# The last group's down projection takes banks of both PSUM pools, and a pair of transfers and tiles is moved at its start

## The chip, the cores and the metric

The kernel runs on one core of a Trainium2 chip. The metric is the device time of one execution in microseconds. TensorE (PE) multiplies, VectorE (DVE), ScalarE (ACT) and GpSimd (POOL) do the rest, and SyncE (SP) issues nearly all transfers. PSUM has eight banks, each of which holds one 128 x 512 product in fp32. Data lies in SBUF with 128 partitions; sizes of tiles below are bytes in one partition.

## The reference, cut to what matters

One layer of a hybrid encoder: 16 meta tokens and 2048 frames, model width 1024. After the mixers (a recurrent part and an attention part) and their output projection `w_o`, the layer ends in a convolutional feed-forward block, which is what the change is about:

```python
h = h + concat([y_rw, y_fx]) @ w_o
h = h + conv_ffn(rmsnorm(h, norm2_g), ffn_w_in, ffn_conv_w, ffn_conv_b, ffn_w_out)

def conv_ffn(x, w_in, conv_w, conv_b, w_out):   # w_in 1024 x 5632, w_out 2816 x 1024
    h = x @ w_in
    y = conv_b + sum(conv_w[i] * shifted(h, 2 - i) for i in range(3))   # causal, by channel
    u, gt = split(y, 2)
    return (silu(gt) * u) @ w_out
```

All is fp32. The kernel writes each operand as a high and a low part in fp32r (`hi` is a cast on ACT, `lo` the difference on DVE or POOL) and multiplies hi x hi, hi x lo and lo x hi, so that each product of 128 x 128 by 128 x 512 is three matmuls.

## The kernel before

The tokens are laid out with features in partitions. The feed-forward block goes by four groups of 512 tokens (`FGROUPS`): `early[0]` and `early[1]` one after the other, and the last two, `a` and `b`, together by a scheme with fewer products (class `Last`). `tail` (L1442) sets the order: `w_o` of `early[1]`, its feed-forward (`F.mlp`), then `w_o(a)`, `half_a`, `w_o(b)`, and `rest()`, which is the last down projection of `early[1]` (L1227): eight products into banks `pr`, each followed by an add on DVE into `acc` (L1237) and by the transfer of that 256 KB piece to the output (L1240).

The last group works on 22 pairs of weight blocks `f`. `Last.up(f)` (L1308) loads two weight tiles `raw` (L1312), makes sums and differences of their quarters (`s1` on POOL, L1342, and three more on POOL, in place), splits them (`qh`, `ql`, L1322 and L1323; `rh`, `rl`, L1348), and forms products of them with seven operands. Of these p1, p2 and ra come from group a alone. p5 (`t1h`, `t1l`), p6 (`t2`), p4 (`t4`), p7 (`t3`), p3 (`b2`) and rb need group b, and `half_b` (L1284) makes them: eight scalings by the norm's factor `rs`, four sums and differences of 128 x 1536, and a cast on ACT and a difference on DVE for each. `rs` comes from a power and a spread on POOL (L1173, L100) and transposes on TensorE (L103). The sums of products are A, B, D and Cb in four banks `pr`; DVE adds them, and the convolution and the gate follow on ACT and DVE (L1338, L1340, L1400, L1402), with the result z split by ACT and POOL (L1404, L1405).

`Last.down` (L1408) multiplies two blocks z by their output weights: 16 products of six matmuls, each into a bank of `self.out` and then added by DVE into `acca` or `accb` (L1423); it is called 11 times, one call for each two `f`, in `Last.mlp` (L1427), behind the matmuls of the next `up`. Its weights use the same `raw` and `qh`, `ql` tiles (two buffers each) as the up projection. In the last call each add is followed by the transfer to the output (L1425).

PSUM is divided into `ffpA`, three banks `pp`, and `ffpR`, five banks `pr`. Before, the last group's up projection has `pr` and its down projection `pp`.

SBUF on the left side is a stack. During the early groups it holds `ffe`, `ffw` (two `ww_raw`, three `ww_hi`, three `ww_lo`, 4096 each), `ffA` (`acc`, 8 x 514 x 4 = 16,448), `ffB` (`xh`, 16,448), `ffC` (`xl`), `ffD`. When they are closed, the same space is given to `ffL0` (late operands of `half_b`: those named in `late_ops`, 6144 each, and `rh`, `rl`, 4096 each), `ffV` (M.W: `raw` first, then `s1`, `qh`, ...), and `ffL1` (the other operands). Group b's attention output lies in `xh` and `xl` (`yB`, L1478) until `w_o(b)` has read it. A tile that gets space of an earlier one waits for all of that one's readers.

Nothing here is ordered by hand alone: the program is traced in the order of the calls, and the scheduler of the language (`schedule_with_timeline_sim=True`, L1550) puts each engine's instructions, and each queue of transfers, in an order that it takes from a simulated timeline. Within an engine and a queue the order is then fixed, and an instruction that waits holds up those behind it.

Of the kernel before, what the change touches and what calls it, by code (L numbers as in the profile page):

```python
# [62 lines left out]
def pools(*args):  # L63

    *ps, where = args
    return lambda shape, tag, bufs=1, dt=F32: ps[where.get(tag, -1)](shape, tag, bufs, dt)
# [1031 lines left out]
class Ffn:  # L1098
# [128 lines left out]
    def down(self, G, fs, zs):  # L1227
        K, nc, acc = self.K, self.K.nc, G.acc
        w = [self.weight(K.fout[f]) for f in fs]
        for m in range(KC):  # L1230
            ms = slice(128 * m, 128 * m + 128)
            for b, nb in G.blocks:
                p = G.out([128, 512])[:, :nb]
                self.product(p, [(wh[:, ms], wl[:, ms], zh[:, b : b + nb], zl[:, b : b + nb])
                                 for (wh, wl), (zh, zl) in zip(w, zs)])
                a = acc[:, m, b : b + nb]
                nc.vector.tensor_tensor(a, a, p, op=ALU.add)  # L1237
            if fs[-1] == FT - 1:
                s = max(16 - G.T0, 0)
                nc.sync.dma_start(K.outT[m, :, G.T0 + s - 16 : G.T0 - 16 + G.n], acc[:, m, s : G.n])  # L1240

    def mlp(self, G, switch=FT, out=None):

# [198 lines left out]
def tail(K, ctx, at, c0):  # L1442

    tc = K.tc
    edge = Pool(tc, ctx, "ffe", side="left")
    late = ExitStack()
    ctx.enter_context(late)
    pA = Pool(tc, ctx, "ffpA", PSUM, side="left")
    bank = lambda shape: pA(shape, "pp", 3)
    turn = ExitStack()  # L1450
    with ExitStack() as c1:
        W = Pool(tc, c1, "ffw", side="left")
        F = Ffn(K, W, (3, 2), edge)
        gA = pools(*(Pool(tc, c1, f"ff{i}", side="left") for i in "ABCD"), {"acc": 0, "xh": 1, "xl": 2})
        cvA = lambda: gA([128, 512], "cv", 5)
        early = [F.group(*g, dict(x=gA, a=gA, z=gA, out=bank, up=bank, ytag="x", abufs=1, parts=WHOLE, small=KC,
                                  cv=cvA, sq=cvA, stage=lambda i: lambda c: cvA())) for g in FGROUPS[:2]]
        early[0].parts = PARTS
        early[0].small = KC // 2
        early[1].small = 0  # L1460
        early[1].last = True
        F.w_o(early[0])
        at(1, False)
        c0.close()
        with ExitStack() as c2:
            attention(K, c2, "at2", [[[2 * i, 2 * i + 1] for i in range(4, 8)]], (1, 4, 2, 352, 2, 0, 0), (2, 2, 1))(0, False)
        pR = Pool(tc, late, "ffpR", PSUM, side="right")
        bankR = lambda shape: pR(shape, "pr", 5)
        F.mlp(early[0])()
        F.w_o(early[1])  # L1470
        rest = F.mlp(early[1], 8, bankR)
        R = Pool(tc, late, "ffR", side="right")
        T = Pool(tc, turn, "ffT", side="right")
        tn = ExitStack()
        N = Pool(tc, tn, "ffN", side="right")
        yA = lambda: [Thirds([R([128, cs.stop - cs.start, 512], f"p{i}", dt=F32R) for i, cs in zip(t, CH3)])
                      for t in ((0, 1, 4), (2, 3, 5))]
        yB = lambda: [gA([128, KC, 514], "x" + t, dt=F32R) for t in "hl"]  # L1478
        a, b = (F.group(*g, dict(x=N, a=R, atag=t, y=y, abufs=1, out=bankR, up=bank, parts=WHOLE, small=KC,
                                 sq=lambda: N([128, 512], "sqv", 1)), win=True)  # L1480
                for g, t, y in zip(FGROUPS[2:], ("acca", "accb"), (yA, yB)))
        M = Last(F, a, b)
        F.w_o(a)
        M.half_a(R, T)
        F.w_o(b)
        rest()

    late_ops = ("t4h", "t4l", "t3h", "t3l", "b2h", "b2l", "rh", "rl")
    L0 = Pool(tc, late, "ffL0", side="left")
    M.W = Pool(tc, late, "ffV", side="left")  # L1490
    L = pools(L0, Pool(tc, late, "ffL1", side="left"), dict.fromkeys(late_ops, 0))
    tn.close()
    with ExitStack() as c1:
        U = Pool(tc, c1, "ffU", side="right")
        M.first = M.up(0)
        next(M.first)
        M.half_b(L, Pool(tc, c1, "ffB", side="left"), T, U)
    turn.close()
    M.C = Pool(tc, late, "ffC2", side="left")
    M.Z = Pool(tc, late, "ffZ", side="right")  # L1500
    M.bank, M.out = bankR, bank
    M.mlp()


# [9 lines left out]
def trunk(tc, args, out, shapes):  # L1514
    K = SimpleNamespace(nc=tc.nc, tc=tc, outT=out, **args)
    with ExitStack() as c0:
        dr = Pool(tc, c0, "scratch", DRAM)
        for name, shape in SCRATCH.items():
            setattr(K, name, dr(list(shape), "d_" + name))
        setup(K, c0)  # L1520
        with ExitStack() as c:
            mixer = ExitStack()
            c.enter_context(mixer)
            at = None
            with ExitStack() as c1:
                def first():
                    nonlocal at
                    mixer.close()
                    at = attention(K, mixer, "at", [[[-1, 0, 1], [2, 3]], [[4, 5], [6, 7]]], (2, 3, 3, 544, 3, 1, 0), (2, 2, 1))
                    at(0, True)  # L1530

                phase1(K, c1, mixer, rwkv, first)
            tail(K, c, at, mixer)
# [21 lines left out]
```

## Time and profile before

| | |
|---|---|
| three timed runs | 3402.91, 3417.93 and 3419.29 us, median 3417.93 |
| profiled execution | 3404.62 us, of which the span of the instructions is 3402.8 us |
| busy share of the span | PE 96%, PEld (weight loads, beside PE) 85%, DVE 69%, ACT 49%, POOL 34% |
| the chain that ended last | PE 48%; DVE 4%; DMA 3% |
| the last group's up and down projections | from about 2662 us to the end |
| transfers of 256 KB to the output | 2.4 to 2.5 us to landing |

The page gives the shares over the whole span; they are averages over stages with different limits. The views by stretch (busy time of each engine, count of its instructions, granted TensorE clock as a share of 2.4 GHz, share and rate of the DMA engines), of waits, and of the timeline show a single stage. In a timeline, consecutive equal instructions are merged; the bracket gives how long the engine was idle before the first of them and what released it.

### The profile page before, as it was taken

Reading aid. Unit: us, or ns where it says so; the run is one execution under the profiler, and the core shown is the slowest. Engines: PE = TensorE matmul, PEld = TensorE weight load, DVE = VectorE, ACT = ScalarE, POOL = GpSimd, SP = SyncE. Lnnn points to the kernel's source line nnn. Section 1 sums busy time; section 2 is a strip of 40 time slices with the busy share of each in tenths; the row PEclk is TensorE's granted clock in tenths of the full one; section 3 lists DMA queues with packets and bytes.
Section 4 is the critical chain, followed back from the end, with each engine's and each line's share of the span. In section 5 each row is a group of like instructions: output and inputs, shape, how many; then the busy total and the mean of one; then the engine's idle time right before and its main releaser. Section 6 shows DMA issues by size and latency. Waiting matters only on the chain.

```text
span 3402.8 us, 61891 instructions
## 1 busy us (share of the span) xinstructions
PE 3275.4 (96%) x23061; PEld 2906.4 (85%) x23061; DVE 2352.7 (69%) x4946; ACT 1664.9 (49%) x3529; POOL 1159.8 (34%) x1733
## 2 busy tenths in 40 slices
PE   7999999999999999999999999999999899999999
PEld 7889888988988988999999998888888677777777
DVE  5665666566556757887878886777665677667666
ACT  5542444554244457765666665654343343334342
POOL 4441112444111157755445453412014422222221
PEclk9999999999999999999999999999999899999999
DMA  4566333356634255333233344324233111111112
GB/s 111 122 133 154 105 93 102 99 121 133 158 88 108 78 172 162 116 107 111 80 89 100 94 130 132 94 73 158 94 98 115 65 50 50 41 53 56 38 50 87
DMA packets 346517, 341.93 MB, mean 100 GB/s; under 512 B 168376, under 2 KB 281256, under 8 KB 345192
## 3 DMA queue, kind: packets, MB, share of 16 engines
q1 hardware_dynamic: 346024, 337.91, 35.1%
q8 instruction: 182, 2.98, 0.4%
q14 instruction: 119, 0.97, 0.1%
q0 software_dynamic: 192, 0.07, 0.0%
HBM read 267.62 MB, written 70.27 MB: 99 GB/s over the span
## 4 chain that ended last, share of the span: by engine, by line
PE 48%; DVE 4%; DMA 3%; ACT 2%; issue 2%; POOL 2%; SPq 0%; ACTq 0%; POOLq 0%; DVEq 0%
PE pp L1121 23%; PE pr L1121 16%; PE o L1031 3%; PE pt L1011 3%; DMA raw<-d_qk 2%; PE s L961 1%; PE s L963 1%; DVE v L1340 1%; DVE rl L1349 1%; DMA raw<-in_fin_dram 1%; POOL kl L903 0%; ACT P L980 0%; ACT ph L1026 0%; DVE ql L89 0%; DVE c L1331 0%
## 5 line engine op out<-in xcount | busy, mean ns | idle before, releaser
L82 DVE TENSOR_TENSOR ww_lo<-ww_raw,ww_hi 128x1024 fp32r<-128x1024 f32 (+1 forms) x172 | 215.5, 1260 | 79.1 <-ACT ww_hi L81 45.0
L1121 PE MATMUL pp<-xh,ww_hi 128*128 128x256 f32 (+2 forms) x1248 | 248.3, 326 | 4.3 <-ACT xh L1186 3.2
L1121 PE MATMUL pp<-xh,ww_lo 128*128 128x256 f32 (+2 forms) x1248 | 250.3, 325 | 0.0
L1121 PE MATMUL pp<-xl,ww_hi 128*128 128x256 f32 (+2 forms) x1248 | 247.9, 324 | 0.0
L81 ACT CAST ww_hi<-ww_raw 128x1024 fp32r<-128x1024 f32 (+1 forms) x172 | 171.4, 1009 | 132.2 <-PE pp L1121 54.9
L1027 DVE TENSOR_TENSOR pl<-pt,ph 128x512 fp32r<-128x512 f32 (+2 forms) x352 | 196.2, 562 | 52.5 <-ACT ph L1026 50.8
L1026 ACT CAST ph<-pt 128x512 fp32r<-128x512 f32 (+2 forms) x352 | 167.6, 485 | 105.1 <-PE pt L1011 73.2
L954 DVE CUSTOM_DVE_ANT_0 P<-cb,s 16x16 f32<-16x16 f32 (+8 forms) x360 | 182.7, 519 | 51.6 <-PE s L963 28.5
L1121 PEld LDWEIGHTS pp<-xh,ww_hi 128*128 128x128 f32 x1248 | 191.2, 189 | 23.9 <-ACT xh L1186 4.5
L1121 PEld LDWEIGHTS pp<-xl,ww_hi 128*128 128x128 f32 x1248 | 194.0, 189 | 17.9
L1121 PEld LDWEIGHTS pp<-xh,ww_lo 128*128 128x128 f32 x1248 | 192.3, 189 | 16.9
L1011 PE MATMUL pt<-cst,P 128*128 128x128 f32 (+2 forms) x1224 | 202.1, 276 | 2.9 <-ACT P L980 1.6
L89 POOL TENSOR_TENSOR wi<-sq,kx 128x320 fp32r<-128x320 f32 (+2 forms) x48 | 48.6, 1012 | 397.7 <-ACT kx L88 296.1
L203 PE MATMUL pj<-xah,w_hi 128*128 128x384 f32 x480 | 166.0, 346 | 1.8 <-ACT xah L194 1.8
L1031 PE MATMUL o<-ph,vs 128*128 128x256 f32 x576 | 158.8, 285 | 6.7 <-ACT ph L1026 6.4
L205 PE MATMUL pj<-xah,w_lo 128*128 128x384 f32 x480 | 164.6, 343 | 0.4 <-DVE r L181 0.4
L204 PE MATMUL pj<-xal,w_hi 128*128 128x384 f32 x480 | 163.6, 341 | 0.0
L1340 DVE SCALAR_TENSOR_TENSOR v<-c,pc,v 128x512 f32<-128x512 f32 x176 | 145.0, 849 | 21.9 <-ACT v L1338 15.3
L1031 PE MATMUL o<-pl,vs 128*128 128x256 f32 x576 | 156.5, 290 | 2.9 <-DVE pl L1027 2.5
L980 ACT ACTIVATE P<-P,nm 128x656 f32<-128x656 f32 (+6 forms) x104 | 143.5, 1380 | 30.7 <-DVE nm L979 30.3
L203 PE MATMUL pj<-xbh,w_hi 128*128 128x320 f32 (+1 forms) x480 | 153.9, 321 | 0.0
L205 PE MATMUL pj<-xbh,w_lo 128*128 128x320 f32 (+1 forms) x480 | 153.8, 320 | 0.0
(501 smaller groups left out, 9859.2 us busy)
## 6 DMA issues: line engine op xcount, KB each, us to landing
ww_raw<-in_fin_dram SPq DMA_DIRECT2D x88, 512.0 KB, 3.6
w_raw<-in_wt_dram SPq DMA_DIRECT2D x60, 512.0 KB, 3.7
ww_raw<-in_fout_dram SPq DMA_DIRECT2D x44, 512.0 KB, 3.7
raw<-in_fin_dram SPq DMA_DIRECT2D x44, 512.0 KB, 3.7
xv<-d_var SPq DMA_DIRECT2D x32, 384.0 KB, 5.9
ww_raw<-in_wo_dram SPq DMA_DIRECT2D x24, 512.0 KB, 3.5
raw<-in_fout_dram SPq DMA_DIRECT2D x44, 256.0 KB, 2.9
raw<-d_qk SPq DMA_DIRECT2D x112, 88.0 KB, 2.6
```

The source lines that it names most:

```text
L81: nc.scalar.copy(hi, raw)
L82: nc.vector.tensor_sub(lo, raw, hi.bitcast(F32))
L203: nc.tensor.matmul(p, wh[:, c, :M], xh[:, c, :n], start=c == 0, stop=False)
L204: nc.tensor.matmul(p, wh[:, c, :M], xl[:, c, :n], start=False, stop=False)
L205: nc.tensor.matmul(p, wl[:, c, :M], xh[:, c, :n], start=False, stop=c == KC - 1)
L954: nc.vector.tensor_tensor_reduce(dst, c, src, 1.0, 3e38, op0=ALU.add, op1=ALU.min, accum_out=mx[:nq, np_ : np_ + 1])
L1011: nc.tensor.transpose(pt[:kn, x, c0 : c0 + nq], P[:nq, k0 : k0 + kn], K.ident[:nq, :nq])
L1026: nc.scalar.copy(ph[:kn, xs, c:N], pt[:kn, xs, c:N])
L1027: nc.vector.tensor_sub(pl[:kn, xs, c:N], pt[:kn, xs, c:N], ph[:kn, xs, c:N].bitcast(F32))
L1031: nc.tensor.matmul(o[:, c:N], vs[:kn, jj], pp[:kn, x, c:N], start=False, stop=jj == nt - 1 and y == 1)
L1121: self.K.nc.tensor.matmul(p, w, x, start=start and i == 0, stop=i == len(mms) - 1, skip_group_check=not start)
L1340: nc.vector.scalar_tensor_tensor(v, t[:, o : o + 512], pcol(K, f"cw{o}", k), v, op0=ALU.mult, op1=ALU.add)
```

## The change

Three edits in the last part of the kernel. The output transfers of the last down projection of the group marked `last` (`early[1]`) are issued by POOL and no longer by SP. `t2l` becomes a late operand: its 6144 bytes go to `ffL0`, so that what is stacked behind `ffL0` moves up by as much, and `ffL1` becomes smaller by as much. The down projection of the last group takes its banks in turn from `pp` and `pr`.

```diff
--- before.py
+++ after.py
@@ -1,3 +1,4 @@
+import itertools
 import math
 from contextlib import ExitStack
 from types import SimpleNamespace
@@ -1237,7 +1238,8 @@
                 nc.vector.tensor_tensor(a, a, p, op=ALU.add)
             if fs[-1] == FT - 1:
                 s = max(16 - G.T0, 0)
-                nc.sync.dma_start(K.outT[m, :, G.T0 + s - 16 : G.T0 - 16 + G.n], acc[:, m, s : G.n])
+
+                (nc.gpsimd if G.last else nc.sync).dma_start(K.outT[m, :, G.T0 + s - 16 : G.T0 - 16 + G.n], acc[:, m, s : G.n])
 
     def mlp(self, G, switch=FT, out=None):
 
@@ -1485,7 +1487,7 @@
         F.w_o(b)
         rest()
 
-    late_ops = ("t4h", "t4l", "t3h", "t3l", "b2h", "b2l", "rh", "rl")
+    late_ops = ("t4h", "t4l", "t3h", "t3l", "b2h", "b2l", "rh", "rl", "t2l")
     L0 = Pool(tc, late, "ffL0", side="left")
     M.W = Pool(tc, late, "ffV", side="left")
     L = pools(L0, Pool(tc, late, "ffL1", side="left"), dict.fromkeys(late_ops, 0))
@@ -1498,7 +1500,9 @@
     turn.close()
     M.C = Pool(tc, late, "ffC2", side="left")
     M.Z = Pool(tc, late, "ffZ", side="right")
-    M.bank, M.out = bankR, bank
+    M.bank = bankR
+    banks = itertools.cycle((bank, bankR))
+    M.out = lambda shape: next(banks)(shape)
     M.mlp()
```

## Rows read from the trace of the kernel before

**Rows 1.** The page, busy us, share of span and instructions.

```profile
PE 3275.4 (96%) x23061; PEld 2906.4 (85%) x23061; DVE 2352.7 (69%) x4946; ACT 1664.9 (49%) x3529; POOL 1159.8 (34%) x1733
```

**Rows 2.** By stretch: length, then busy (count) PE PEld DVE ACT POOL, clock, DMA.

```profile
2661.80:2703.30 41.50, 26.57 (x83) 19.53 (x82) 32.47 (x34) 16.32 (x23) 20.36 (x12) 0.75 0.19 63
2703.30:3398.50 695.20, 673.64 (x2890) 542.62 (x2888) 497.38 (x732) 269.08 (x467) 170.51 (x210) 1.00 0.16 53
```

**Rows 3.** Waits from 2700 on: who <- for whom: us, times, longest.

```profile
PE pp L1121 <- DVE acca L1423: 20.9, 10, 3.1
...
ACT qh L1322 <- PE pp L1121: 12.4, 10, 1.4
```

**Rows 4.** Timeline of PE at one such wait: start, length, what.

```profile
2817.27 0.73 PE L1121 MATMUL pp<-zh,qh 128*128 128x512 f32 x2 [3.09 <-DVE acca L1423]
...
2818.34 1.05 PE L1121 MATMUL pp<-zh,ql 128*128 128x512 f32 x2
2819.19 1.05 PE L1121 MATMUL pp<-zh,qh 128*128 128x512 f32 x2
```

**Rows 5.** Timeline of DVE beside it.

```profile
2810.00 1.28 DVE L1331 TENSOR_TENSOR c<-c,pr 128x512 f32<-128x512 f32 x2
...
2814.26 0.68 DVE L1331 TENSOR_TENSOR c<-c,pr 128x512 f32<-128x512 f32 x1
...
2816.55 0.67 DVE L1423 TENSOR_TENSOR acca<-acca,pp 128x512 f32<-128x512 f32 x1
```

**Rows 6.** Line 1423: ns min/median/max, first and last start.

```profile
L1423 DVE TENSOR_TENSOR acca<-acca,pp x88: 671/680/690, 2750.7 to 3397.1; 128x512 f32<-128x512 f32 x88
```

**Rows 7.** Timeline of SP from 2600 to 2680.

```profile
2651.72 10.93 SPq L1240 DMA_DIRECT2D out_dram<-acc  x8
2664.94 0.82 SPq L1312 DMA_DIRECT2D raw<-in_fin_dram  x2
```

**Rows 8.** SP's waits, 2550 to 2760.

```profile
SPq L1312 <- DMA out_dram<-acc: 2.0, 1, 2.0
```

**Rows 9.** PE's waits, 2655 to 2705.

```profile
PE pr L1121 <- ACT qh L1322: 7.3, 1, 7.3
```

**Rows 10.** Timeline of all engines before the last group.

```profile
2647.52 2.06 PE L1121 MATMUL pr<-xh,ww_lo 128*128 128x512 f32 x8
...
2658.04 1.02 POOL L1173 TENSOR_TENSOR r<-r,mhalf 128x4 f32<-128x4 f32 x1 [5.63 <-DVE r L1172]
...
2659.14 0.62 POOL L100 TENSOR_SCALAR E<-r 128x512 f32<-128x512 f32 x1
...
2661.17 0.59 PEld L103 LDWEIGHTS pp<-cst,E 128*128 128x128 f32 x4
...
2662.20 4.03 DVE L1273 SCALAR_TENSOR_TENSOR b<-accb,pc,pp 128x512 f32<-128x512 f32 x6
```

**Rows 11.** Line 282, transfers issued by POOL: ns min/median/max.

```profile
L282 POOL DMA_DIRECT2D d_fl<-st x6: 520/647/785, 49.9 to 671.1; - x6
```

**Rows 12.** DVE by group, 2661.8 to 2703.3: busy, mean ns, idle before.

```profile
L1323 DVE TENSOR_TENSOR ql<-raw,qh 128x384 fp32r<-128x384 f32 x8 | 4.9, 652 | 6.1 <-PE pr L1121 6.1
...
L1268 DVE TENSOR_TENSOR t1l<-xs,t1h 128x1536 fp32r<-128x1536 f32 x1 | 3.4, 3401 | 0.5 <-ACT t1h L1267 0.5
L1294 DVE TENSOR_TENSOR xs<-xs,t 128x1536 f32<-128x1536 f32 x1 | 2.6, 2552 | 0.0
...
L1268 DVE TENSOR_TENSOR t3l<-b,t3h 128x1536 fp32r<-128x1536 f32 x1 | 1.7, 1744 | 0.0
...
L1323 DVE TENSOR_TENSOR ql<-s,qh 128x384 fp32r<-128x384 f32 x2 | 1.7, 844 | 1.5 <-ACT qh L1322 1.5
...
L1349 DVE TENSOR_TENSOR rl<-raw,rh 128x256 fp32r<-128x256 f32 x2 | 0.8, 416 | 0.0
```

**Rows 13.** Timeline of DVE, the last of group b's operands.

```profile
2690.02 1.74 DVE L1268 TENSOR_TENSOR t4l<-xs,t4h 128x1536 fp32r<-128x1536 f32 x1
```

**Rows 14.** Tile `s`, 2655 to 2760: ns min/median/max.

```profile
L1342 POOL TENSOR_TENSOR s<-raw x4: 1009/1161/6675, 2670.0 to 2748.4; 128x384 f32<-128x384 f32 x4
```

## The prediction

> **What bounds the kernel now.** I read the page's engine shares first: TensorE is busy for 96% of the span [rows 1], so a change gains where TensorE stands still or runs at its lower clock, and hardly anywhere else. The table by stretch then shows two places around the change [rows 2]. In the 41.5 us from 2661.8 TensorE is busy for 26.6 us, at a mean granted clock of 0.75. In the 695.2 us after it TensorE is busy for 673.6 us at 1.00, and each of the 2890 matmuls counted there takes 0.233 us of that. The reader is to see one large loss, and one of 21.6 us that is spread.
>
> The waits of that long stretch name the spread one [rows 3]: 20.9 us in 10 waits are a product for `pp` that waits for a DVE add into `acca`. The timeline of one shows what it is. Three products of the down projection are done, one in each `pp` bank, at 2814.2; the fourth starts at 2817.27, after 3.09 us [rows 4]. DVE runs adds, convolutions and weight splits of the up projection from 2810.0 on, and comes to the first of the three evictions at 2816.55 [rows 5]. It is no lack of DVE throughput: DVE is busy for 497.4 of the 695.2 us [rows 2], and a cycle of 16 products needs 16 x 0.68 = 10.9 us of DVE [rows 6] against 16 x 6 x 0.233 = 22.4 us of TensorE. It is a lack of banks while DVE is busy elsewhere for 6.6 us.
>
> The large loss lies at the start of the last group. The loads of its first weights are issued at 2664.94, behind eight output transfers on SP that follow the adds one by one [rows 7], and after a wait of 2.0 us for an output to land [rows 8]. That wait is an overlay: the ring `ffw` has 8 tiles of 4096 B a partition, `acc` behind it 16,448 B, and so ends at 49,216 B; the eight late operands take 6 x 6144 + 2 x 4096 = 45,056 B of the same space, so that the first `raw` tile begins inside `acc`. TensorE stands for 7.3 us until the first cast of these weights [rows 9], and 14.9 - 7.3 = 7.6 us more in the stretch [rows 2], for operands of group b.
>
> **The change part by part.** *Banks.* A product has the same six matmuls and one add whichever bank it is in: no instruction is added or removed, and 88 of 176 products move to `pr`. At 2814 most of `pr` is free: the up projection uses four of its five banks at most, and those read by the adds at 2810.0 and 2814.26 [rows 5] are let go. So TensorE has room for at least six products, 8.4 us from about 2808.5, instead of three, and DVE comes to evict inside that. Bounds: a gain of 20.9 us [rows 3] and some 2 us for about ten matmuls after the longest wait that ran at the lower level of 1.2 GHz (a step of 0.43 us, [rows 4]); on the other side a loss, since half of the products stand in banks that the up projection needs (rival 3). I take -20, near the first end: no wait is over 3.1 us, and the room added is over 4 us.
>
> *Outputs on POOL.* Eight issues leave SP and join POOL's queue, each waiting there for its add, one in about 1.4 us. Behind them can stand what makes group b's scale, a power at 2658.04 and a spread at 2659.14 that ends at 2659.8; TensorE takes the spread at 2661.17 [rows 10]. So 1.4 us of delay is covered, and what is over goes into the end. The trace shows no such issue from 128 partitions; the nearest are six from 8 partitions at 0.52 to 0.79 us [rows 11]. Below, 0.52 us: nothing shows, since the adds are 1.4 us apart. Above, if it went with the partitions, 16 x 0.65 = 10.4 us each, 83 us on POOL, and the scale behind half of them, 40 us late. I take 0.8 us, by the nearest row, and no cost. SP has nothing else that is late there.
>
> The Trainium skill ("SBUF — State Buffer", the three doors, the "DVE blocks DMA" trap) says that a DMA issued from POOL cannot be prepared while DVE holds the port pair that the two share, and advises SP or ACT. No run here shows an output issued from POOL, and the six issues of [rows 11] do not show the stall. What it would do is rival 2.
>
> *Loads and overlay.* With `t2l` among them the late operands take 51,200 B, past the end of `acc`, so `raw` now lies on `xh`, whose last reader is the last product of `w_o(b)`, run of 2647.52 to 2649.6 [rows 10]. Today the first product follows the issue by 2661.8 + 7.3 - 2664.9 = 4.2 us [rows 7, 9], so it could come at 2653.8. Then 24 matmuls (w1 p1, w2 p2, wu ra: 5.6 us) that need nothing of group b can run from 2661.8 on, where TensorE idles. What is late next is group b on DVE: eight scalings from 2662.2 (4.03 us for six, [rows 10]), a difference of 1.75 us and a cast of, say, 1.5 us, so t1h at about 2670.8. The gain is read from DVE's chain up to its last operand, t4l, which ends at 2691.8 [rows 13]. By the means of [rows 12] it loses 3 x 0.65 + 2 x 0.42 + 0.84 = 3.6 us of weight splits, which then lie among the adds before 2661.8 (0.69 us in 1.4 us); 1.5 + 0.5 = 2.0 us of waits; and (3.40 - 1.74) + (2.55 - 1.74) = 2.5 us by which two of its instructions are stretched while POOL works beside them (POOL's own `s1` takes 6.68 us there, median 1.16, [rows 14]). That is 8.1 us. By the order of first use `b2h` moves up onto `acc` and has a new wait, for the last output: issued by 2662.7, landed by 2664.9 now [rows 7], about 0.8 us later from POOL; its operand is scaled only at 2666.2, so nothing. All casts stand behind it on ACT. Bounds: nothing, if the scale or this cast slips by as much; and 15 us, if of the 41.5 us only 87 x 0.233 = 20.3 us of matmuls, 3.4 us before t1h and 3 us elsewhere remain. I take -8.
>
> **Sum.** The profiled execution took 3404.62 us (the span of 3402.8 and 1.8 around it). 3404.6 - 20 - 8 = 3376.6. The three timed runs are 3402.9, 3417.9 and 3419.3: the profile agrees with the lowest, and the median stands 13.3 us above it. Nothing in the trace says at which of these two levels the changed kernel's median will be, so I put the forecast half-way, 8 us over the sum: **3385 us**.
>
> **The rivals.** *1. The stall moves.* DVE's work for the up projection still comes in one lump, and the wait shows up at the next weights: ACT casts `qh` of the up projection only when the down products have let go of it (12.4 us of ACT in 10 waits, [rows 3]). For: the two waits come in equal number. Against: between such a cast and its use TensorE has eight products, 11 us. If three quarters come back, -5 - 8: 3391.6, on the middle level 3400.
>
> *2. POOL holds the outputs back.* Each issue waits for a DVE instruction as well, `acc` comes free late, and `b2h`, with every cast behind it on ACT, slips by what the loads win: -20 alone, 3384.6, on the middle level 3393. For: POOL and DVE do stretch each other [rows 12, 14]. Against: those are long instructions on tiles in SBUF, and the adds before 2661.8 are short.
>
> *3. Slower: the up projection waits for banks.* Down products sit in `pr` until DVE's lump is over, and the next A, B or Cb finds none free. Today no wait of TensorE for `pr` is among the long ones of [rows 3]. It costs from 28 us on, 2.8 us in each of ten cycles; with two waits of 2.5 us a cycle it is 50 - 20 - 8 = +22: 3426.6, on the middle level 3435. Against: DVE empties a bank in half the time in which TensorE fills it, and eight banks hold one lump.
>
> *4. It does not do what it says:* the scheduler, which orders each engine's work by a simulated timeline, leaves loads and products where they are: 3404.6, on the middle level 3413.
>
> **How the numbers follow.** Forecast 0.53, rival 1 0.17, rival 2 0.13, rival 3 0.09, rival 4 0.08. About 0.5% (17 us) is what a measurement of this kernel can tell from no change, so faster means under 3400.8. That holds for nearly all of the forecast, half of rival 1 and most of rival 2: 0.70. Slower, over 3435, is half of rival 3 and a little of a large POOL price: 0.07. The rest is 0.23. The range goes from 3363 (both gains near their upper ends, on the lower level: 3404.6 - 23 - 15 = 3366.6, and 0.1% of scatter) to 3415, which takes in rivals 1, 2 and 4.
>
> **What would show it.** Right: TensorE's waits for `pp` fall from 10 to two or fewer and none for `pr` takes their place; the first weights' loads are issued before 2651; the 7.3 us before the first `qh` product fall under 1 us; t4l ends near 2684; and from 2661.8 to the end the kernel is 28 us shorter. Wrong: TensorE waits for `pr` on a DVE add; POOL issues over 1.4 us; a `b2h` cast after 2668. The prediction fails as a whole if the adds before 2661.8 come late, or if the long stretch still takes 690 us.

## The result, and the profile after

The changed kernel takes **3375.26 us** (median of four runs, 3372.55 to 3383.06) against 3418.61 us for the kernel before (four runs: the three of the table ahead of the prediction, 3402.91 to 3419.29, and one more of 3423.53): a ratio of 0.9885, interval 0.9849 to 0.9921. The profiled execution took 3372.55 us against 3404.62 us, 32.1 us less. The forecast was 3385 us, and its sum for the profile's own level 3376.6.

Every view below is read as its counterpart ahead of the prediction; lines of the source stand one further down up to 1237, two from 1240 on. The page's row of all engines, for [rows 1]:

```profile
PE 3263.8 (97%) x23061; PEld 2899.1 (86%) x23061; DVE 2346.5 (70%) x4946; ACT 1665.7 (49%) x3529; POOL 1174.9 (35%) x1741
```

The table by stretch, for [rows 2]. The borders are moved so that the same work lies between them: the second begins at the second pair's first product and holds the same 2890 matmuls.

```profile
2660.97:2698.16 37.19, 23.99 (x84) 17.67 (x84) 27.46 (x28) 14.17 (x18) 24.73 (x16) 0.72 0.18 55
2698.16:3366.40 668.24, 668.15 (x2890) 542.31 (x2888) 491.85 (x734) 268.93 (x468) 174.08 (x209) 1.00 0.17 55
```

The second stretch lost 695.20 - 668.24 = **27.0 us**. TensorE stood for 21.6 us of it before and for 0.1 us now; the other 5.5 us are busy time of the same matmuls, most of it at the edges of the stands; the part on why the prediction was right takes it apart. The first stretch lost 41.50 - 37.19 = **4.3 us**: 1.7 us less standing, 2.6 us less busy time. With 0.8 us by which the whole stage began earlier the 32.1 us are accounted for.

TensorE's waits from 2640 to the end, all that there are; for [rows 3] and [rows 9]:

```profile
PE pr L1122 <- ACT t1h L1269: 8.6, 1, 8.6
PE pr L1122 <- DVE t1l L1270: 3.5, 1, 3.5
PE pr L1122 <- ACT c L1363: 0.8, 1, 0.8
PE pr L1122 <- ACT t4h L1269: 0.2, 1, 0.2
```

No product waits for a bank, neither `pp` nor `pr`. The wait for `qh` is gone, but a wait for `t1h` of 8.6 us stands in its place: the start lost little.

The cycle of [rows 4] and [rows 5], first on TensorE (first product, and the first that needs a bank of `pp` again), then on DVE:

```profile
2800.55 0.63 PE L1122 MATMUL pp<-zh,qh 128*128 128x512 f32 x2
...
2811.95 0.63 PE L1122 MATMUL pp<-zh,qh 128*128 128x512 f32 x2
```

```profile
2806.22 0.79 DVE L1351 TENSOR_TENSOR rl<-raw,rh 128x256 fp32r<-128x256 f32 x1
2806.93 0.67 DVE L1425 TENSOR_TENSOR acca<-acca,pp 128x512 f32<-128x512 f32 x1
2807.53 0.91 DVE L1402 SCALAR_TENSOR_TENSOR v<-c,v 128x512 f32<-128x512 f32 x1
2808.36 0.41 DVE L1351 TENSOR_TENSOR rl<-raw,rh 128x256 fp32r<-128x256 f32 x1
```

Two things changed. A bank is needed again 11.4 us after the first product, where before it was needed after about 5.7 us and TensorE stood from 2814.2 on. And the first bank is free earlier too, 7.05 us after the first product (2806.93 + 0.67) against 8.8 us before: the scheduler put an add between the two splits `rl`, which both stood ahead of it before [rows 5]. This is the cycle with the longest wait; over all ten cycles the first bank is free 5.9 to 8.8 us after the first product before and 5.9 to 7.5 us now. By either order that is in time for a need after 11.4 us: by this count the number of banks alone would do in the change.

The start on SP, POOL, TensorE and DVE, for [rows 7], [rows 10] and [rows 13]; the first row is the first of the eight products at which the stage is taken to begin. Its counterpart before:

```profile
2649.41 0.63 PE L1121 MATMUL pr<-zh,ww_hi 128*128 128x512 f32 x2
```

And the change:

```profile
2648.58 0.63 PE L1122 MATMUL pr<-zh,ww_hi 128*128 128x512 f32 x2
2648.77 42.32 SPq L1314 DMA_DIRECT2D raw<-in_fin_dram  x4
...
2652.54 0.56 POOL L1242 DMA_DIRECT2D out_dram<-acc  x1 [0.35 <-DVE acc L1238]
...
2659.32 0.15 DVE L1173 TENSOR_SCALAR r<-pp 128x4 f32<-128x4 f32 x1
...
2660.26 1.03 POOL L1354 TENSOR_TENSOR raw<-s,raw 128x384 f32<-128x384 f32 x1
...
2660.56 1.56 PE L1122 MATMUL pr<-p,qh 128*128 128x512 f32 x6
2661.23 1.04 POOL L1174 TENSOR_TENSOR r<-r,mhalf 128x4 f32<-128x4 f32 x1
...
2662.24 1.14 POOL L1242 DMA_DIRECT2D out_dram<-acc  x2
...
2663.39 1.02 POOL L1355 TENSOR_TENSOR raw<-raw 128x384 f32<-128x384 f32 x1
...
2664.37 0.63 POOL L101 TENSOR_SCALAR E<-r 128x512 f32<-128x512 f32 x1
...
2666.16 0.60 PE L104 MATMUL pp<-cst,E 128*128 128x128 f32 x4
2666.80 4.04 DVE L1275 SCALAR_TENSOR_TENSOR b<-accb,pc,pp 128x512 f32<-128x512 f32 x6 [0.73 <-PE pp L104]
...
2675.38 1.65 PE L1122 MATMUL pr<-t1h,qh 128*128 128x512 f32 x3 [8.62 <-ACT t1h L1269]
...
2685.42 1.75 DVE L1270 TENSOR_TENSOR t4l<-xs,t4h 128x1536 fp32r<-128x1536 f32 x1
```

The loads go out with the stage's first product, and TensorE runs into the last group's matmuls without a gap. But group b's scale is late. Counted from the stage's first product, the scalings begin 18.2 us in; before it was 2662.20 - 2649.41 = 12.8 us [rows 10].

### The profile page after: what moved, and what is told of

Its sections match the earlier page's. It is cut to its first block, busy times and chain, and to the rows that moved or that the text cites. A ratio compares the mean times of both kernels' runs of the same rounds, so it can differ in the third digit from the quotient of the medians.

```text
span 3370.7 us, 61910 instructions
## 1 busy us (share of the span) xinstructions
PE 3263.8 (97%) x23061; PEld 2899.1 (86%) x23061; DVE 2346.5 (70%) x4946; ACT 1665.7 (49%) x3529; POOL 1174.9 (35%) x1741
## 4 chain that ended last, share of the span: by engine, by line
PE 49%; DMA 3%; DVE 3%; POOL 2%; issue 2%; ACT 2%; SPq 0%; POOLq 0%; ACTq 0%; DVEq 0%
PE pr L1122 22%; PE pp L1122 19%; PE o L1032 2%; DMA raw<-d_qk 2%; PE pt L1012 2%; PE s L962 1%; PE s L964 1%; POOL kl L904 1%; DVE P L955 0%; DVE pl L1028 0%; DVE ww_lo L83 0%; ACT ph L1027 0%; DMA cb<-d_cd 0%; SPq L902 0%; POOL kq L907 0%
## 5 line engine op out<-in xcount | busy, mean ns | idle before, releaser
L1342 DVE SCALAR_TENSOR_TENSOR v<-c,pc,v 128x512 f32<-128x512 f32 x176 | 144.3, 844 | 21.6 <-ACT v L1340 14.5
```

The lines of the kernel that those rows point to most:

```text
L1342: nc.vector.scalar_tensor_tensor(v, t[:, o : o + 512], pcol(K, f"cw{o}", k), v, op0=ALU.mult, op1=ALU.add)
```

## The experiments

All go by the medians and by one more number, since the medians scatter by several us: the **last stage**, from its first product to the end of the span of the profiled execution. The profiled executions of all the kernels begin it between 2644.95 and 2660.92 us, a scatter ahead of the lines that the edits change (only the fourth bank of its own also takes a bank from the early groups), whose cause I did not look for. The kernel before was profiled once, so its 753.4 us are one execution. The change was measured a second time, to see how well that number repeats:

> The change itself once more, on the same chip as the two: 722 us from the first product of the last down projection of early[1] to the end; both theories expect its time within 5 us of 3375 us.

| kernel | median (runs) | ratio to before, interval | last stage |
|---|---|---|---|
| before | 3406.8 to 3418.6 by set | 1 | 753.4 |
| the change | 3375.26 (4) | 0.9885, 0.9849 to 0.9921 | 722.1 |
| the change again | 3377.62 (4) | 0.9910, 0.9897 to 0.9923 | 722.1 |
| banks alone | 3380.71 (4) | 0.9916, 0.9888 to 0.9943 | 725.8 |
| start alone | 3400.54 (10) | 0.9963, 0.9947 to 0.9980 | 754.7 |
| without `t2l` | 3381.71 (4) | 0.9917, 0.9893 to 0.9941 | 726.1 |
| outputs on SP | 3370.25 (4) | 0.9884, 0.9860 to 0.9909 | 719.0 |
| outputs on SP again | 3368.34 (4) | 0.9869, 0.9845 to 0.9894 | 720.4 |
| + first weights on DVE | 3374.31 (4) | 0.9891, 0.9855 to 0.9927 | 719.8 |
| + difference first | 3373.27 (6) | 0.9901, 0.9884 to 0.9919 | 721.5 |
| + both | 3369.73 (4) | 0.9894, 0.9881 to 0.9907 | 721.5 |
| every third product in `pr` | 3374.93 (1) | | 720.9 |
| all products in `pr` | 3384.11 (1) | | 721.4 |
| a fourth bank of its own | 3381.94 (1) | | 724.3 |

The change's last stage repeats within 0.1 us.

**Banks alone**: outputs back on SP, `t2l` no late operand.

```diff
-                (nc.gpsimd if G.last else nc.sync).dma_start(...
+                nc.sync.dma_start(...
-    late_ops = (..., "rh", "rl", "t2l")
+    late_ops = (..., "rh", "rl")
```

> The banks in turn alone; outputs on SP and t2l where it was. Theory (the gain is nearly all banks: 26 us of TensorE's waits in the long stretch, some 4 us at the start of the last group): span 3370.7 + 4 = 3375 us, no wait of TensorE for pp from 2705 on, and the 7.3 us before the first product of the last group as before. Rival (the earlier start carries the gain, or both edits are needed together): span over 3390 us.

Of the change's 31.3 us in the last stage 27.6 us are there. The start is as before: the loads leave at 2665.04 behind the overlay, and the wait for `qh` is back. The longest of TensorE's waits, and SP's row:

```profile
PE pr L1122 <- ACT qh L1324: 7.2, 1, 7.2
```

```profile
2665.04 0.81 SPq L1314 DMA_DIRECT2D raw<-in_fin_dram  x2
```

**Start alone**: all down products in `pp`.

```diff
-    banks = itertools.cycle((bank, bankR))
+    banks = itertools.cycle((bank,))
```

> Outputs on POOL and t2l moved; the down projection in pp alone. Theory: the ten waits of 2 to 3 us for pp come back, span 3402.8 - 4 to 5 = 3398 us; the first product 7 us earlier than before, but the scale of group b (the power on POOL) some 4 us later, so that the last operand ends only 5 to 6 us earlier. Rival (the start is worth 20 us or more): span under 3385 us.

The start is that of the change (scalings 18.2 us in, t4l 36.8 us in, in both), and the ten waits for `pp` are back. Its two longest waits, and its table by stretch over the same 2890 matmuls:

```profile
PE pp L1122 <- DVE acca L1425: 21.7, 10, 3.0
PE pr L1122 <- ACT t1h L1269: 8.6, 1, 8.6
```

```profile
2698.60:3401.00 702.40, 679.91 (x2890) 546.69 (x2888) 496.76 (x733) 269.21 (x468) 172.81 (x210) 0.99 0.16 52
```

This execution gained some 6 us ahead of the 2890 matmuls (754.7 - 702.4 = 52.3 us against 753.4 - 695.2 = 58.2 us) and lost 7.2 us in them, of which 679.91 - 673.64 = 6.3 us is busy time: the granted clock of the stretch is 0.99 instead of 1.00, and after some waits more matmuls run at the lower level, as here at 3141 us (granted clock 0.50 from 3141.4 to 3144.5; two matmuls in 1.05 us, 0.63 us later on):

```profile
3141.39 1.22 PE L1122 MATMUL pp<-zh,qh 128*128 128x512 f32 x2 [2.29 <-DVE acca L1425]
3142.41 1.05 PE L1122 MATMUL pp<-zl,qh 128*128 128x512 f32 x2
...
3144.77 0.63 PE L1122 MATMUL pp<-zl,qh 128*128 128x512 f32 x2
```

That execution is the slowest of the kernel's ten; by the medians the start alone gave 0.4%, some 12 us, more than its own stretch shows. Which is typical stays open; it also means that ten such waits can cost some 7 us more than they did in the one profile of the kernel before.

**Without `t2l`**: outputs on POOL, but `raw` begins inside `acc` again.

```diff
-    late_ops = (..., "rh", "rl", "t2l")
+    late_ops = (..., "rh", "rl")
```

> The change without t2l: the first weight tile begins inside acc again, with the outputs on POOL. Theory (overlay): the first loads wait for the last output to land, 2665 to 2667 us, and the start is no earlier than before: TensorE idle 7 us or more before the first product, span 3374 to 3378 us. Rival (only the queue on SP mattered): loads at 2649 us, span 3371 us.

SP's queue holds no output any more, and still the loads go out late. The waits of SP, its load, and two rows of POOL:

```profile
SPq L1314 <- DMA out_dram<-acc: 30.0, 2, 28.6
```

```profile
2669.51 0.80 SPq L1314 DMA_DIRECT2D raw<-in_fin_dram  x2
```

```profile
2661.59 0.54 POOL L1242 DMA_DIRECT2D out_dram<-acc  x1 [0.85 <-DVE acc L1238]
2662.14 1.05 POOL L1174 TENSOR_TENSOR r<-r,mhalf 128x4 f32<-128x4 f32 x1
```

So it is the overlay that held the loads, not the queue. The rows of POOL also give the price of the outputs there in pure form: the issues take 0.54 to 0.69 us, and the power of the scale starts 8.67 us into the stage against 8.63 us before. Outputs on POOL delay nothing as long as the loads are late.

**Outputs on SP**, with `t2l` late, that is the overlay's edit alone beside the banks.

```diff
-                (nc.gpsimd if G.last else nc.sync).dma_start(...
+                nc.sync.dma_start(...
```

> The change with the outputs left on SP. Theory (queue): the two loads are issued behind the eighth output, at 2662 us, with no wait for landing, so the first product comes at about 2667; the power for group b's scale runs some 4 us earlier than in the change, as POOL has no outputs. The two about cancel: span 3370 to 3375 us. Rival (the scheduler moves the loads ahead of the outputs once nothing overlays): loads at 2649 us and the scale early, span 3366 us.

The rival had the mechanism: once nothing in the overlay holds them, the scheduler puts the loads ahead of the outputs in SP's queue (the stage begins at 2654.74 here). That the span, 3373.7 us, fell into the theory's band is due to that late beginning.

```profile
2654.93 0.80 SPq L1314 DMA_DIRECT2D raw<-in_fin_dram  x2
2657.04 10.93 SPq L1242 DMA_DIRECT2D out_dram<-acc  x8
```

With POOL rid of the issues the power starts 9.95 us in instead of 12.65 us, the scalings 15.65 us instead of 18.2 us; 13 early matmuls, not 24, stand ahead of the transposes. Again, against scatter:

> The same edit as in the run before it with the outputs back on SP and t2l among the late operands, to tell a difference of 3 us from scatter. From the first product of the last group to the end of the span the change took 722.1 us in two profiled executions, this edit 719.0 us in one. If the transfers on POOL cost the start 3 us, as the later scale in the trace of the change says (the power behind POOL's weight sums and outputs), the stretch takes 719.0 +- 0.5 us again and the first up-projection product on t1h waits about 7.0 us, not 8.6. If it was scatter between executions, the stretch takes 721 to 723 us. In whole times 3 us is less than the scatter of the medians: about 0.9885 +- 0.003 either way.

719.0 and then 720.4 us: neither the one account's band nor the other's. In both executions the chain of group b is the same to 0.01 us (scalings 15.65 us in, t4l 35.21 us in against 36.84 us in the change); the second ran some matmuls at the lower clock level (granted clock 0.50) that the first ran at the higher one (1.00). Three of them, in the first execution and then in the second:

```profile
2691.51 0.85 PE L1122 MATMUL pr<-t2l,qh 128*128 128x512 f32 x3
```

```profile
2685.18 1.49 PE L1122 MATMUL pr<-t2l,qh 128*128 128x512 f32 x3
```

So 1.6 us are the outputs', by t4l (36.84 - 35.21), and the rest of the 1.7 to 3.1 us is how soon the clock rises.

**First weights on DVE**, on top of that: the sum and three differences of the first pair's weights leave POOL.

```diff
-        nc.gpsimd.tensor_tensor(s1, a21, a22, op=ALU.add)
+        eng = nc.gpsimd if f else nc.vector
+        eng.tensor_tensor(s1, a21, a22, op=ALU.add)
...                                   # and the three differences likewise
```

> Outputs on SP and, for the first weights of the last group alone, the four sums and differences of their quarters on DVE instead of POOL. Theory (group b's scale is late because the power and the spread stand behind those four on POOL): the spread is there 3 to 4 us earlier, TensorE's wait for t1h falls from 7 to 4 us, span 3 us below the kernel with the outputs on SP. Rival (the scale is late because its transposes stand behind the 24 early products on TensorE, or its first step behind the adds on DVE): wait for t1h and span unchanged within 1 us.

The power follows its input after 0.2 us instead of 0.3 us: with the outputs on SP, POOL's sums hardly held it any more. And the transposes stand behind 16 early matmuls of TensorE instead of 13, and the scalings begin 16.4 us in, later than the 15.65 us without the edit; TensorE waits 7.8 us for t1h, not 7.0 us. No gain.

**Difference first**: in `half_b` the difference for `t1h` goes ahead of the last scalings; alone, and with the edit before it.

```diff
-        nc.vector.tensor_sub(b11, b12, b11)
+        first = nc.vector.tensor_sub(b11, b12, b11)
+        with self.F.K.tc.issue_after(first.ins):
+            self.half_b_rest(P, S, U, b11, b21, b12, b22)
...                                   # half_b_rest: what stood behind it, as it was
```

> Outputs on SP, and in half_b the difference for p5 is put ahead of the five scalings that DVE now runs before it. Theory (what is left of the loss at the start is DVE's order: the first operand of group b waits for scalings that it does not need): TensorE's wait for t1h falls from 7.0 to 3 to 4 us and that for t1l from 3.5 to under 2 us; from the first product of the last down projection of early[1] to the end 714 us instead of 719. Rival (DVE's chain to its last operand sets the start, whatever comes first): the waits move to later operands and the 719 us stay within 1.

> The same with the first weights' sums and differences on DVE instead of POOL. As these on DVE alone changed the wait for t1h by less than 1 us, the theory expects no more than 1 us beside the kernel without them (713 to 715 us); the rival (POOL's work stretches DVE's chain) expects 2 us less.

The cast of t1h starts 20.4 us in instead of 23.65 us, and the wait for it falls from 7.0 to 3.7 us; t4l stays 35.21 us in, and TensorE waits for `t4h` instead (all waits of the first of the two):

```profile
PE pr L1122 <- ACT t4h L1269: 5.3, 1, 5.3
PE pr L1122 <- ACT t1h L1269: 3.7, 1, 3.7
PE pr L1122 <- DVE t1l L1270: 1.8, 1, 1.8
PE pr L1122 <- ACT c L1368: 0.8, 1, 0.8
```

It is DVE's whole chain for group b that bounds the start, not its first link: TensorE stands for 11.6 us in all in the first run, against 11.7 us in the first without the edit. The last stage, 721.5 us in both runs, is in neither account's band (714, and 719 within 1). What it took beyond 719.0 and 720.4 us is busy time of TensorE: it ran at a granted clock of 0.50 for 20.5 us there, against 13.6 us in both executions with the outputs on SP. Whether the edit or scatter made the clock rise later stays open.

**How many banks, and whose**: three kernels, each timed once.

```diff
-    banks = itertools.cycle((bank, bankR))
+    banks = itertools.cycle((bank, bank, bankR))           # every third in pr
+    banks = itertools.cycle((bankR,))                      # all in pr
+    banks = itertools.cycle((bank, bank, bank, fourth))    # pr with 4 banks, one taken from it
```

> The change with every third product in pr instead of every second (bank, bank, bankR). Theory (only the number of free banks counts while DVE is busy for 6.6 us): room for four products instead of six, so that the ten waits stay at about half: 8 to 15 us in all, span 3380 to 3386 us. Rival (any outlet to pr ends the waits, as the scheduler then reorders DVE): no waits, span 3371 us.

> The change with the down projection in pr alone, so that both projections share five banks and pp is idle. Theory (number of free banks): two or three of the five are free in DVE's lump, so ten waits of 2 to 4 us again, now for pr, span 3390 to 3400 us. Rival (the third rival of the prediction, the up projection starves when the down products hold its banks): waits also in front of the up projection's products, over 40 us in all, span over 3410 us.

> A fourth bank of its own for the down projection, taken from the up projection, which has exactly the four it uses (also the early groups go with four): no bank is shared. Theory (number of free banks): room for four products, waits of about half, 8 to 15 us in all; span 3380 to 3390 us. Rival (sharing by turns is what helps): as before the change, 20 us of waits, span 3392 us or more.

My count of banks, at DVE's order of before, failed in all three: the ten waits come back in none. All products in `pr`, with three banks of the eight idle, have no wait for a bank. Its DVE at the same cycle, whose first product stands at 2811.35:

```profile
2816.60 0.42 DVE L1351 TENSOR_TENSOR rl<-raw,rh 128x256 fp32r<-128x256 f32 x1
2816.93 0.68 DVE L1425 TENSOR_TENSOR acca<-acca,pr 128x512 f32<-128x512 f32 x1
```

The first add comes 5.6 us after the first product. With a fourth bank it is 6.2 us, and two short waits are left:

```profile
PE pp L1122 <- DVE acca L1425: 0.7, 1, 0.7
...
PE pp L1122 <- DVE accb L1425: 0.2, 1, 0.2
```

In each of these the scheduler put an add earlier on DVE (8.1 us before, in this cycle). How much of the gain is the order and how much the bank can be estimated for the fourth bank. Four banks need a free one after 4 x 1.4 us and 1.4 us for six other matmuls = 7.0 us. At DVE's order of before, where the first bank was free after 7.5 to 8.8 us in nine of the ten cycles, they would have waited 0.5 to 1.8 us in each of the nine, 9 us in all, instead of 20.9; measured are 0.9 us. By this count some 12 us there are the bank's and some 8 us the order's, which came with the banks. The order alone, at three banks, was not tried, so how far it would go by itself is not shown.

## Why the prediction was right, point by point

*Banks: right, and sized too small.* Forecast -20, bound -23; measured -27.0 (the 2890 matmuls) and, alone, 753.4 - 725.8 = 27.6. All 20.9 us of waits went. I gave the matmuls behind them 2 us in the bound and nothing in the term; the busy time fell by 5.5 us. The lower level, which the bound counted, is the smaller part: of the ten waits only the longest has it behind it [rows 4], with eight steps of 0.40 to 0.43 us where others take 0.23, 1.5 us in all. The rest lies mostly at the edges of the stands, which I had not counted. Before each of the 12 stands (ten for `acca`, two short ones) the last matmul counts its whole 0.40 us, where in a stream the next one starts after 0.23, and the first step behind it takes 0.1 us longer: about 0.28 us a stand, 3.4 us in all. A stand of the kernel before without the lower level (six matmuls in 1.56 us are 5 x 0.23 + 0.40; two take 0.73 us behind it, elsewhere 0.63):

```profile
2879.96 1.56 PE L1121 MATMUL pp<-zh,ql 128*128 128x512 f32 x6
2883.85 0.73 PE L1121 MATMUL pp<-zh,qh 128*128 128x512 f32 x2 [2.32 <-DVE acca L1423]
```

The busy column of [rows 2] had the whole sum: 673.64 / 2890 = 0.2331 us each, where 668.15 / 2890 = 0.2312 us was to be had.

*Why a bank was free: half right.* The room is there as worked out. That DVE's order would change with it was not foreseen; it gave 1.7 us more in the cycle shown and less in the others. The change does not need it (11.4 us of room against 8.8 us at the most); the run with four banks does.

*Start: right sign, too small, and this is the step that failed.* The forecast was -8, measured -4.3 in the change and 725.8 - 722.1 = 3.7 us against banks alone. In three other executions whose scalings and t4l come at the same places (start alone, every third product and all products in `pr`) the start is 1.6 us shorter, so -5.9: TensorE ran at a granted clock of 0.50 for 13.6 us there and for 20.5 us in the change and its repetition. The chain inside group b did what was said: from the first scaling to t4l it took 2690.02 - 2662.20 = 27.8 us before [rows 10, 13] and takes 2685.42 - 2666.80 = 18.6 us, 9.2 us less (forecast 8.1). The 8.1 counted three splits `ql` of raw weights, and five stood in that chain; with all five it is about 9.4 us. They are, in the kernel before:

```profile
2670.81 1.02 DVE L1323 TENSOR_TENSOR ql<-raw,qh 128x384 fp32r<-128x384 f32 x2
2684.46 2.29 DVE L1323 TENSOR_TENSOR ql<-raw,qh 128x384 fp32r<-128x384 f32 x3
```

What failed is the cover: "So 1.4 us of delay is covered, and what is over goes into the end." Only the eight issues were held against it, at a price that was right (0.8 taken; 0.54 to 0.69 measured). But with the loads 16 us earlier the first weights' own work comes early as well, and stands ahead of the scale. On DVE and POOL: counted within the stage, the input of the power is 2.35 us late (splits of weights before it), the power another 1.7 us (an output and a difference of weights on POOL), and the spread 2.0 us more behind it (two outputs and a difference); it ends 16.4 us in, before 10.4 us [rows 10]. On TensorE: the 24 early matmuls, which I had put where TensorE idles, stand in its order ahead of the transposes, 24 x 0.233 = 5.6 us. The transposes' weights are loaded 17.35 us in, in the change, in its repetition (where the spread ends 15.8 us in) and in the start alone, before 11.76 us in. So both hold the scale, TensorE's order last, which is why taking the work off POOL did not help. The scalings come 5.4 us late, and 9.2 - 5.4 = 3.8 us is what was left at t4l.

*What I said each step would show.* The loads before 2651: 2648.77. The wait for `qh` gone: yes. t4l's end near 2684: 2687.2, wrong by the late scale. A cast of `b2h` after 2668 was to show the prediction wrong: it came at 2670.87, but released by DVE's scaling, not by an output; that cover held. 28 us from 2661.8 on: 31.3 us.

*The overlay: right.* The run without `t2l` shows it with a wait of SP for an output that is no longer in its queue. Outputs on POOL are not what freed the loads, and cost 1.6 us of the start; the version without that edit is the fastest measured, 3368.34 and 3370.25 us, but its interval reaches into the change's.

*The rivals.* That the stall moves was wrong for the banks and right for the start (from `qh` to `t1h`: 14.9 us of standing became 13.2). That POOL holds the outputs back did not show: the Trainium skill's "DVE blocks DMA" trap ("SBUF — State Buffer", "SBUF: two separate sides") speaks of issues beside DVE operations that hold the shared ports. No run shows whether the DVE operations beside these eight issues hold them; the issues took 0.54 to 0.69 us, like the six of [rows 11], and no stall shows. That the up projection waits for banks is refuted in its strongest form by all products in `pr`. That nothing happens is refuted by the table.

*The levels.* I added 8 us for the two levels of the runs before. In the profiled executions of the changed kernels the scatter is mostly ahead of the last stage (it begins between 2644.95 and 2660.92) and not the change's; of the kernel before there is one profile, so what makes its two levels is not shown. Without the 8 us the sum was 4 us over the profiled execution: 7.0 us too little for the banks, 3.7 us too much for the start, 0.8 us of an earlier stage. That it came so close is in part luck, since the first two errors offset each other.

## What to carry to other kernels

What a periodic wait costs is read from the busy time of the engine as much as from its waits: each stand adds busy time at its two edges (0.28 us here), behind some the granted clock falls to 0.50 (one of the ten before, five in the start alone), and the sum is in the count and busy columns of the same stretch. When loads come earlier, everything that they release comes earlier too and takes its place in queues: list those instructions on every engine ahead of the next critical one before the gain is booked. A scheduler that is given one more buffer may also reorder the engine that empties it, so redo a count of buffers with the order read anew.

## What was not expected of the hardware

A split of 128 x 1024 on POOL took 16.03 us while DVE worked through its chain of 128 x 1536 operations beside it without a pause; before it took 2.69 us, and it was a DVE operation beside it (t1l) that took 3.40 us instead of 1.75. The split of the change ended 2.2 us after DVE's last such operation (t4l, at 2685.42 + 1.75 = 2687.17), so nearly the whole of a split like the one before came after the chain. The same holds in all eleven runs with this split beside the chain: 14.4 to 17.0 us, its end 2.2 to 2.3 us behind t4l. No engine waits for its result here, but on the path its 13 us more would have outweighed what the start gained three times. First the kernel before, then the change:

```profile
2677.75 2.69 POOL L1268 TENSOR_TENSOR rl<-xs,rh 128x1024 fp32r<-128x1024 f32 x1
2678.66 3.40 DVE L1268 TENSOR_TENSOR t1l<-xs,t1h 128x1536 fp32r<-128x1536 f32 x1 [0.46 <-ACT t1h L1267]
```

```profile
2673.38 16.03 POOL L1270 TENSOR_TENSOR rl<-xs,rh 128x1024 fp32r<-128x1024 f32 x1 [7.84 <-ACT rh L1269]
```
